# A feed-forward layer with block products for more of its columns: gate by seven products, up plain and turned, sums chained in PSUM

## The chip, the core and the metric

One core of a Trainium2 chip runs the kernel. Five engines work in parallel, each with its own queue: TensorE (PE) does matmuls, VectorE (DVE) and ScalarE (ACT) elementwise work, GpSimd (POOL) little else than transfers here, SyncE (SP) issues the other transfers. PEld is PE's loading of weights into the array. The metric is device time in microseconds (us) for one execution; smaller is better.

## The reference

256 tokens with 1024 features pass a decoder block: a gated linear recurrence and an attention, each projected, multiplied by a sigmoid gate and added, then an output projection and a SwiGLU feed-forward layer with 2816 hidden columns. The change touches the branch gates and the feed-forward layer:

```python
    gates = jax.nn.sigmoid(gl.reshape(B, S, N_BRANCH, D))      # gl: 2048 columns of h @ w_in
    merged = gates[:, :, 0, :] * y_hg + gates[:, :, 1, :] * y_at
    x = x + merged @ w_out[l]
    h2 = rmsnorm(x, ffn_norm_g[l])
    x = x + (jax.nn.silu(h2 @ w_ffn_gate[l]) * (h2 @ w_ffn_up[l])) @ w_ffn_down[l]
```

All inputs are float32.

## The kernel before

**Three matmuls for one.** A float32 product is made of fp32r parts. Every weight chunk of 128 x 2048 floats (1 MB) comes by SP into `wraw` (or a `W` tile), ACT casts it to `whi` (L55), DVE subtracts to get the rest, `wlo` (L56). PE then adds activation-high x whi, activation-high x wlo and activation-low x whi. `wraw`, `whi` and `wlo` have three buffers each (pool `wp`), used in turn by all chunks of the kernel, so the chunk after next is the furthest that can be prepared.

**Two layouts of a product.** *Feature-major* (`feat_steps`, L101 to L105): weights stand in the array, the tokens stream; high and low parts of the activations stream in one matmul of 512 columns, plus one of 256 with wlo. The result has features on partitions, as the down projection needs it; low and high sums are folded by an ACT copy of 256 and a DVE add of 256 (`fold`, L121 and L122). *Token-major*: activations stand in the array, 512 weight columns stream; the result has tokens on partitions, and for the down projection it is transposed on PE (`turn`, four transposes a quarter) and split again.

**Seven products instead of eight** (`scheme`). Tokens are cut into two halves of 128, the 1024 inputs into two of 512, 1024 columns into two of 512. A product of 2 x 2 blocks takes seven block products instead of eight, with sums of token blocks (`token_sums2`) and of weight quarters W11, W12, W21, W22 (DVE rows of 128 x 2048: L841, L848, L853, L859). A block product is 12 matmuls (L645). The results are added into the quarters `q(i, j)` by DVE.

**The feed-forward layer before.** 22 tiles of 128 hidden columns. Tiles 0 to 13 (`NPL = 14`) are plain and feature-major, in blocks of 4, 4, 4 and 2 (`plain`, gate then up, half of the 1024 inputs a step). Tiles 14 to 21 go by `scheme`: the gate's seven products stand between the steps of the plain blocks, up's seven products between the down blocks. A down block (`down_steps`, L903 to L905) takes two tiles of the hidden layer: one 1 MB chunk of w_down and 24 matmuls into four PSUM banks that add up over eleven blocks.

**The order of work.** A scheduler that builds the program places each instruction on its engine's queue; `tc.issue_after` ties a step to the last matmul of the step before it (`step`), so PE's order is that of the code. DVE and ACT get their rows in the order that the scheduler found. The branch gates are made in the same way earlier, by a `scheme` written out by hand (L701 to L735) between the steps of `at_block`.

Of the kernel before, what the change touches and what calls it, by code (L numbers as in the profile page):

```python
# [7 lines left out]
F32 = mybir.dt.float32  # L8
# [3 lines left out]
OP = mybir.AluOpType  # L12
# [15 lines left out]
def tile_hgrn2_moba_block(ctx: ExitStack, tc: tile.TileContext, xm, xw, table, runs,  # L28
# [666 lines left out]
    def gq(i, j):  # L695
        return G[0][:, i, j * 512:(j + 1) * 512]
# [4 lines left out]
    nc.scalar.copy(gq(1, 0), b1)  # L701
# [3 lines left out]
    at = then(product, b3, summed(0), halves(W11), True)  # L705
    W22 = quarter(1, 1, "T8")
# [4 lines left out]
    put_oT(halved[-1][0], low)  # L711
    b2 = pa("b2")
    at = then(product, b2, summed(1), halves(W11), True)
    W21 = quarter(1, 0, "T2")
    at = then(product, b1, tokens(0, 1), halves(W21), False)
    sigmoid(0, 0, b1)
    step1, out1 = at_block(1)
    at = then(step1)
    with tc.issue_after(halved[-1][1].ins):
        out0()  # L720
        nc.vector.tensor_add(gq(0, 1), b2, gq(1, 0))
    at = then(product, b2, summed(2), halves(W12), False)
    nc.vector.tensor_add(gq(1, 1), b2, gq(1, 0))
    nc.vector.tensor_add(gq(1, 1), gq(1, 1), b3)
# [55 lines left out]
    NPL = 14  # L780
    SC = NPL * P

    def token_sums2():
        C = big.tile([P, 4, 4, P], F32, name="C2", tag="T3")
        hi = big.tile([P, 4, 4, P], F32R, name="C2h", tag="T4")
        lo = big.tile([P, 4, 4, P], F32R, name="C2l", tag="T5")
        nc.vector.tensor_add(C[:, 0], x2f[:, 0, :, P:S], x2f[:, 1, :, P:S])
        nc.vector.tensor_sub(C[:, 1], C[:, 0], x2f[:, 0, :, 0:P])
        nc.vector.tensor_sub(C[:, 2], x2f[:, 0, :, 0:P], x2f[:, 0, :, P:S])
        nc.vector.tensor_sub(C[:, 3], x2f[:, 1, :, 0:P], C[:, 1])  # L790
# [8 lines left out]
    def plain(f0, nf, b):  # L799
        cw = nf * P  # L800
        pg = [pw() for _ in range(nf)]
        steps = feat_steps(pg, w_gate, f0 * P, x2T, cw)
        next(steps)
        yield
        next(steps)
        zt = big.tile([P, 4, S], F32, name="zt", tag=("T12", "T13")[b % 2])
        for j in range(nf // 2):
            z = zt[:, 2 * j:2 * j + 2, :]
            for i in range(2):
                fold(z[:, i, :], pg[2 * j + i])  # L810
# [9 lines left out]
        hT = big.tile([P, nf, 2, S], F32R, name="hT", tag=("T7", "T2", "T3", "T12")[b])  # L820
        for j in range(nf // 2):
            js = slice(2 * j, 2 * j + 2)
            for i in range(2 * j, 2 * j + 2):
                fold(fl[:, i, :], pu[i])
            nc.vector.tensor_mul(zt[:, js, :], zt[:, js, :], fl[:, js, :])
            split(zt[:, js, :], hT[:, js, 0, :], hT[:, js, 1, :])
        for j in range(nf):
            hk.append((f0 + j, hT, j))
        yield

    def scheme(w, banks, p1, at_out, q):
# [8 lines left out]
        nc.scalar.copy(p1, b1)  # L840
# [5 lines left out]
        b3 = banks()  # L846
# [6 lines left out]
        nc.vector.tensor_sub(W12, W22, W12)  # L853
# [20 lines left out]
    def down_steps():  # L874
        (fa, act, ja), (fb, act_b, jb) = hk[2 * chunk[0]:2 * chunk[0] + 2]
        assert fb == fa + 1 and act is act_b
# [4 lines left out]
        for tb in range(2):  # L881
            for half in range(2):
                ts = slice(tb * P, (tb + 1) * P)
                cs = slice(half * 512, (half + 1) * 512)
                if end and tb == 1 and half == 1:
                    for c0, cw in ((512, 256), (768, 256)):
                        bank = pw()
                        for i in range(2):
                            j = ja + i
                            for m, w in ((0, hi), (0, lo), (1, hi)):  # L890
                                tail[0] = nc.tensor.matmul(bank[:, 0:cw], act[:, j, m, ts], w[:, i, c0:c0 + cw],
# [7 lines left out]
                for i in range(2):  # L899
                    j = ja + i  # L900
                    st = n == 0 and i == 0
                    en = i == 1 and n == NFT // 2 - (2 if tb == 1 and half == 1 else 1)
                    nc.tensor.matmul(acc[tb][half], act[:, j, 0, ts], hi[:, i, cs], start=st, stop=False)  # L903
                    nc.tensor.matmul(acc[tb][half], act[:, j, 0, ts], lo[:, i, cs], start=False, stop=False)  # L904
                    tail[0] = nc.tensor.matmul(acc[tb][half], act[:, j, 1, ts], hi[:, i, cs], start=False, stop=en)  # L905
# [14 lines left out]
    sG = big.tile([P, 2, D], F32, name="sG", tag="T6")  # L920

    def gq2(i, j):
        return sG[:, i, j * 512:(j + 1) * 512]

    def silu(i, j, src):
        nc.scalar.activation(gq2(i, j), src, AF.Silu, scale=r2[:, i:i + 1])

    ring = iter([pa, ph, pa])
    blocks = iter([c for b in range(3) for c in [plain(4 * b, 4, b)]])
    chunks_a = (c for g in blocks for c in g)  # L930
    gate = scheme(w_gate, lambda: next(ring)("g"), gq2(1, 0), silu, gq2)
    third, chunk_no = None, 0
    for what in "cccsPcPccPcPccPcPcPc":
        if what == "c":
            with tc.issue_after(x2_split[0].ins), tc.issue_after(x2_split[1].ins):
                step(next, chunks_a) if chunk_no == 2 else None
            if chunk_no != 2:
                step(next, chunks_a)
            third = third or (halved[-1] if chunk_no == 2 else None)
            chunk_no += 1  # L940
            continue
        with tc.issue_after(third[0].ins), tc.issue_after(third[1].ins):
            if what == "P":
                step(next, gate)
            else:
                sums2 = token_sums2()
    assert not list(chunks_a) and not list(gate)
    rest = plain(12, 2, 3)
    for _ in range(4):
        step(next, rest)  # L950

    U = None
    hq = [None, None]

    def uq(i, j):
        return U[:, i, j * 512:(j + 1) * 512]

    def hidden(i, j, src):
        nc.vector.tensor_mul(uq(i, j), src, gq2(i, j))

    def turn(i, j):
        bank = pw("turn")
        src = uq(i, j)
        for k in range(4):
            tail[0] = nc.tensor.transpose(bank[:, k * P:(k + 1) * P], src[:, k * P:(k + 1) * P], ident)
        ts = slice(i * P, (i + 1) * P)
        split(bank.rearrange("p (k t) -> p k t", k=4), hq[j][:, :, 0, ts], hq[j][:, :, 1, ts])

    acc = [[ph("acc00"), ph("acc01")], [pa("acc10"), pa("acc11")]]
    p1u = big.tile([P, 512], F32, name="p1u", tag="T15")  # L970
    up = scheme(w_up, pw, p1u, hidden, uq)
    step(down)
    step(next, up)
    step(down)
    U = big.tile([P, 2, D], F32, name="U", tag="T7")
    step(next, up)
    step(down)
    step(next, up)
    step(down)
# [11 lines left out]
    parts = down_steps()
    for k in range(4):
        step(next, parts)
        if k == 2:
            step(turn, 0, 1)
    assert not list(parts)
    for j in (1, 0):
        for k in range(4):
            hk.append((NPL + 4 * j + k, hq[j], k))
    step(turn, 1, 0)  # L1000
    for _ in range(4):
        step(down)
# [45 lines left out]
```

## Time and profile before

| | |
|---|---|
| median of 3 runs | 490.17 us (490.13 to 490.63) |
| the profiled execution | 490.14 us |
| its span in the profile | 488.4 us |
| TensorE clock granted | 1.00 throughout |
| matmul instructions in the profile | 2598 |
| DMA | 91.16 MB, mean 187 GB/s |

The profile gives the busy time of each engine, a chain of work that ended last, and groups of instructions with their count, their busy time, the mean of one in ns, and the idle time of the engine ahead of them with what ended it. L12 is line 12 of the kernel. In rows by window there stand, for each engine, its busy time and the count of its instructions, then the granted clock, the share of DMA and GB/s. The feed-forward layer runs from about 305 us to the end.

### The profile page before, as it was taken

Reading aid. Unit: us, or ns where it says so; the run is one execution under the profiler, and the core shown is the slowest. Engines: PE = TensorE matmul, PEld = TensorE weight load, DVE = VectorE, ACT = ScalarE, POOL = GpSimd, SP = SyncE. Lnnn points to the kernel's source line nnn. Section 1 sums busy time; section 2 is a strip of 40 time slices with the busy share of each in tenths; the row PEclk is TensorE's granted clock in tenths of the full one; section 3 lists DMA queues with packets and bytes.
Section 4 is the critical chain, followed back from the end, with each engine's and each line's share of the span. In section 5 each row is a group of like instructions: output and inputs, shape, how many; then the busy total and the mean of one; then the engine's idle time right before and its main releaser. Section 6 shows DMA issues by size and latency. Waiting matters only on the chain.

```text
span 488.4 us, 6511 instructions
## 1 busy us (share of the span) xinstructions
PE 483.1 (99%) x2598; PEld 406.7 (83%) x2598; DVE 397.8 (81%) x426; ACT 301.7 (62%) x402; POOL 25.2 (5%) x59
## 2 busy tenths in 40 slices
PE   8999999999999999999999999999999999999997
PEld 7888888888888888988888878888888888888885
DVE  5769999697779989499987767899998779986843
ACT  5887656767748984875564445886566576444520
POOL 1930320000000000000000000000000000000000
PEclk9999999999999999999999999999999999999999
DMA  8977695624524348418267577715395664242402
GB/s 314 401 240 253 196 299 187 224 87 158 190 83 158 134 139 269 166 46 299 90 233 281 172 260 260 251 37 183 128 338 179 178 250 171 92 173 86 172 1 86
DMA packets 42142, 91.16 MB, mean 187 GB/s; under 512 B 1656, under 2 KB 3960, under 8 KB 42112
## 3 DMA queue, kind: packets, MB, share of 16 engines
q1 hardware_dynamic: 41376, 88.11, 52.5%
q0 software_dynamic: 736, 2.65, 1.7%
q8 instruction: 20, 0.33, 0.3%
q14 instruction: 10, 0.08, 0.1%
HBM read 89.67 MB, written 1.07 MB: 186 GB/s over the span
## 4 chain that ended last, share of the span: by engine, by line
PE 96%; DVE 2%; DMA 1%; issue 0%; ACT 0%
PE pw L102 16%; PE pw L84 10%; PE pw L85 10%; PE pw L86 10%; PE pw L168 5%; PE pw L105 4%; PE acc L903 4%; PE acc L905 4%; PE acc L904 4%; PE pw L101 4%; PE pw L645 4%; PE b L645 4%; PE g L645 3%; PE pw L684 1%; PE pw L685 1%; PE pw L683 1%
## 5 line engine op out<-in xcount | busy, mean ns | idle before, releaser
L56 DVE TENSOR_TENSOR wlo<-wraw,whi 128x2048 fp32r<-128x2048 f32 (+1 forms) x69 | 148.9, 2163 | 37.7 <-ACT whi L55 37.4
L55 ACT CAST whi<-wraw 128x2048 fp32r<-128x2048 f32 (+1 forms) x69 | 124.8, 1813 | 62.1 <-PE pw L86 25.2
L102 PE MATMUL pw<-x2T,whi 128*128 128x512 f32 x224 | 71.8, 395 | 0.0
L55 ACT CAST whi<-W 128x2048 fp32r<-128x2048 f32 x21 | 40.2, 1915 | 28.5 <-PE acc L905 13.6
L84 PE MATMUL pw<-whi,XT 128*128 128x512 f32 x144 | 56.9, 395 | 0.0
L56 DVE TENSOR_TENSOR wlo<-W,whi 128x2048 fp32r<-128x2048 f32 x21 | 47.9, 2286 | 10.2 <-ACT whi L55 10.1
L86 PE MATMUL pw<-whi,XT 128*128 128x512 f32 x144 | 56.2, 390 | 0.0
L85 PE MATMUL pw<-wlo,XT 128*128 128x512 f32 x144 | 56.1, 390 | 0.0
L102 PE MATMUL pw<-XT,whi 128*128 128x512 f32 x128 | 40.6, 395 | 0.0
L102 PEld LDWEIGHTS pw<-x2T,whi 128*128 128x128 f32 x224 | 35.0, 189 | 0.4
L86 PEld LDWEIGHTS pw<-whi,XT 128*128 128x128 f32 x144 | 27.0, 188 | 5.7
L84 PEld LDWEIGHTS pw<-whi,XT 128*128 128x128 f32 x144 | 27.0, 188 | 5.6
L105 PE MATMUL pw<-x2T,wlo 128*128 128x256 f32 x112 | 31.3, 279 | 0.3 <-DVE wlo L56 0.3
L85 PEld LDWEIGHTS pw<-wlo,XT 128*128 128x128 f32 x144 | 27.1, 188 | 5.4
L101 PE MATMUL pw<-x2T,wlo 128*128 128x256 f32 x112 | 31.2, 279 | 0.0
L105 PEld LDWEIGHTS pw<-x2T,wlo 128*128 128x128 f32 x112 | 21.1, 188 | 5.2 <-DVE wlo L56 0.7
L101 PEld LDWEIGHTS pw<-x2T,wlo 128*128 128x128 f32 x112 | 21.0, 188 | 5.0
L903 PE MATMUL acc<-whi,hT 128*128 128x512 f32 x56 | 21.9, 391 | 0.0
L905 PE MATMUL acc<-whi,hT 128*128 128x512 f32 x56 | 21.8, 390 | 0.0
L904 PE MATMUL acc<-wlo,hT 128*128 128x512 f32 x56 | 21.8, 389 | 0.0
L102 PEld LDWEIGHTS pw<-XT,whi 128*128 128x128 f32 x128 | 19.8, 189 | 0.2
L168 PE MATMUL pw<-whi,XT 128*128 128x512 f32 x64 | 17.6, 393 | 0.3 <-ACT whi L182 0.3
(357 smaller groups left out, 1019.9 us busy)
## 6 DMA issues: line engine op xcount, KB each, us to landing
wraw<-w_in SPq DMA_DIRECT2D x26, 1024.0 KB, 5.1
wraw<-w_down SPq DMA_DIRECT2D x11, 1024.0 KB, 5.0
wraw<-w_gate SPq DMA_DIRECT2D x6, 1024.0 KB, 5.1
wraw<-w_up SPq DMA_DIRECT2D x6, 1024.0 KB, 5.1
wraw<-w_at SPq DMA_DIRECT2D x4, 1024.0 KB, 6.6
W<-w_in SPq DMA_DIRECT2D x4, 1024.0 KB, 5.2
wraw<-w_hg SPq DMA_DIRECT2D x4, 1024.0 KB, 6.6
W<-w_gate SPq DMA_DIRECT2D x4, 1024.0 KB, 6.1
```

Of the source, the lines that this page charges most:

```text
L55: high = nc.scalar.copy(hi, src)
L56: return high, nc.vector.tensor_sub(lo, src, hi.bitcast(F32))
L84: nc.tensor.matmul(ps[tb], part(act, kt, 0)[:, ts], wh, start=(kt == 0), stop=False)
L85: nc.tensor.matmul(ps[tb], part(act, kt, 0)[:, ts], wl, start=False, stop=False)
L86: nc.tensor.matmul(ps[tb], part(act, kt, 1)[:, ts], wh, start=False, stop=(kt == KT - 1))
L101: nc.tensor.matmul(ps[ct][:, 0:S], lo[:, i, cs], part(act, kt, 0), start=False, stop=False)
L102: wide = nc.tensor.matmul(ps[ct], hi[:, i, cs], both, start=(kt == 0), stop=(kt == KT - 1))
L105: tail[0] = nc.tensor.matmul(ps[ct][:, 0:S], lo[:, i, cs], part(act, kt, 0), start=False, stop=False)
L168: nc.tensor.matmul(ps[tb], part(XT, kt, am)[:, tb * P:(tb + 1) * P], w[:, i, hs], start=(kt == 0 and am == 0 and w is wh), stop=(kt == KT ...
L645: mm = nc.tensor.matmul(bank, act(kt, m), h[:, kt, :], start=(first and kt == 0 and m == 0 and h is hi), stop=(kt == 3 and m == 1), skip_g ...
L903: nc.tensor.matmul(acc[tb][half], act[:, j, 0, ts], hi[:, i, cs], start=st, stop=False)
L904: nc.tensor.matmul(acc[tb][half], act[:, j, 0, ts], lo[:, i, cs], start=False, stop=False)
```

## The change

*Branch gates.* The same seven products at the same places. Two of them now add onto a PSUM bank that still holds an earlier product (`b1`, with `first` False), and ACT copies the bank out between; DVE has three adds in place of five, ACT two copies more.

*Feed-forward layer.* Plain and feature-major are now tiles 0 to 5 (`NPL = 6`, blocks of 4 and 2). Tiles 6 to 13 ("B", 1024 columns): gate by `scheme`, up plain but token-major (`up_plain`, four token blocks of 24 matmuls), multiplied (`times`) and turned (`turn`). Tiles 14 to 21 ("A"): gate and up by `scheme`, as before, but gate too now stands among the down blocks, and runs of up to three products stand between two down blocks ("PdPPdPPPdP", "PdPPPdP").

*The scheme itself.* The sums of weights and tokens have other signs, so that b1 adds up over products 4, 6 and 7 (`summed(1)`, `summed(2)`, `tokens(1, 1)`); three weight sums on DVE (W11+W12 L841, W11+W22 L852, W21+W11 L860) in place of four, three adds into q in place of five. W12+W22 is made by an adding transfer on POOL's queue (L842), which reads W22 from HBM a second time. Signs are put right in the scale of Silu (`r2n`) and in a multiply with -1 (L934).

```diff
-    NPL = 14
+    NPL = 6
...
-    def scheme(w, banks, p1, at_out, q):
+    def scheme(w, c0, bank, at_out, q):
...
         product(b1, tokens(0, 0, X), halves(W11), True)
-        nc.scalar.copy(p1, b1)
-        nc.vector.tensor_sub(W11, W12, W11)
+        nc.scalar.copy(q(0, 0), b1)
+        nc.vector.tensor_add(W11, W11, W12)
+        nc.gpsimd.dma_start(W12, w[512:D, c0 + 512:c0 + D].rearrange("(k p) c -> p k c", p=P), accum_op=OP.add)
         yield
-        product(b1, tokens(0, 1, X), halves(W21), False)
-        at_out(0, 0, b1)
+        b2 = bank("b2")
+        product(b2, tokens(0, 1, X), halves(W21), True)
+        nc.vector.tensor_add(q(0, 0), q(0, 0), b2)
+        at_out(0, 0, q(0, 0))
         yield
...
         product(b3, summed(0, sums2), halves(W11), True)
-        nc.vector.tensor_sub(W11, W22, W11)
+        nc.scalar.copy(q(1, 1), b3)
+        nc.vector.tensor_add(W11, W11, W22)
         yield
-        b2 = banks()
-        product(b2, summed(1, sums2), halves(W11), True)
-        nc.vector.tensor_add(q(0, 1), b2, p1)
-        nc.vector.tensor_sub(W12, W22, W12)
-        yield
-        product(b2, summed(2, sums2), halves(W12), False)
-        nc.vector.tensor_add(q(1, 1), b2, p1)
-        nc.vector.tensor_add(q(1, 1), q(1, 1), b3)
-        at_out(1, 1, q(1, 1))
-        nc.vector.tensor_sub(W21, W21, W11)
+        product(b1, summed(1, sums2), halves(W11), False)
+        nc.scalar.copy(q(0, 1), b1)
         yield
         product(b3, summed(3, sums2), halves(W22), False)
         nc.vector.tensor_add(q(0, 1), q(0, 1), b3)
         at_out(0, 1, q(0, 1))
+        nc.vector.tensor_add(W21, W21, W11)
         yield
-        product(b2, tokens(1, 1, X), halves(W21), False)
-        nc.vector.tensor_add(q(1, 0), b2, p1)
-        at_out(1, 0, q(1, 0))
+        product(b1, summed(2, sums2), halves(W12), False)
+        nc.vector.tensor_add(q(1, 1), q(1, 1), b1)
+        at_out(1, 1, q(1, 1))
+        yield
+        product(b1, tokens(1, 1, X), halves(W21), False)
+        at_out(1, 0, b1)
         yield
...
+    def up_plain(c0, q):
+        for j in range(2):
+            ps = [pw(), pw()]
+            for kt, wh, wl in chunks(w_up, c0 + j * 512, 512, (4, 4)):
+                for tb in range(2):
+                    ts = slice(tb * P, (tb + 1) * P)
+                    nc.tensor.matmul(ps[tb], part(x2T, kt, 0)[:, ts], wh, start=(kt == 0), stop=False)
+                    nc.tensor.matmul(ps[tb], part(x2T, kt, 0)[:, ts], wl, start=False, stop=False)
+                    tail[0] = nc.tensor.matmul(ps[tb], part(x2T, kt, 1)[:, ts], wh, start=False, stop=(kt == KT - 1))
+                if kt == 3:
+                    yield
+            for tb in range(2):
+                nc.scalar.copy(q(tb, j), ps[tb])
+            yield
...
+    step(next, second_c)
+    step(next, second_c)
+    step(next, gate)
+    UB = quarters("UB", "T7")
+    up_b = up_plain(FB * P, UB)
+    step(next, up_b)
+    step(next, gate)
...
+    for what in "PdPPdPPPdP":
+        step(*((down,) if what == "d" else (next, gate)))
...
+    for what in "PdPPPdP":
+        step(*((down,) if what == "d" else (next, up)))
+    hA1 = turned2(FA + 4, "T2")
+    hA0 = turned2(FA, "T3")
+    step(turn, UA, 0, 0, *hA0, banks["b2"])
+    step(next, up)
+    step(turn, UA, 0, 1, *hA1)
+    step(down)
+    step(turn, UA, 1, 1, *hA1, banks["b3"])
```

How this moves rows is seen in the order of the built programs. First place: DVE's queue in the first gate scheme, from the wlo of its third product on (before: `wlo_2986`; W00 to W11 are the quarters W11 to W22, zt the folded gate of a plain block):

```order
L56 TENSOR_TENSOR wlo_2986<-W00_2793,whi_2985 128x2048
L56 TENSOR_TENSOR wlo_3008<-wraw_3006,whi_3007 128x2048
L122 TENSOR_TENSOR zt_2971<-pw_2891,zt_2971 128x256
L122 TENSOR_TENSOR zt_2971<-pw_2892,zt_2971 128x256
L122 TENSOR_TENSOR zt_2971<-pw_2893,zt_2971 128x256
L811 TENSOR_TENSOR zt_2971<-zt_2971,R2_2636 128x512
L122 TENSOR_TENSOR zt_2971<-pw_2894,zt_2971 128x256
L848 TENSOR_TENSOR W00_2793<-W11_2799,W00_2793 128x2048
```

The changed kernel, from the wlo of the third product (`wlo_2951`) to that of the first token block of up (`wlo_2973`) and one further:

```order
L56 TENSOR_TENSOR wlo_2951<-W00_2795,whi_2950 128x2048
L56 TENSOR_TENSOR hT_2862<-zt_2729,hT_2862 128x2x256
L852 TENSOR_TENSOR W00_2795<-W00_2795,W11_2801 128x2048
L122 TENSOR_TENSOR zt_2942<-pw_2896,zt_2942 128x256
L122 TENSOR_TENSOR zt_2942<-pw_2897,zt_2942 128x256
L56 TENSOR_TENSOR wlo_2973<-wraw_2971,whi_2972 128x2048
L810 TENSOR_TENSOR zt_2942<-zt_2942,R2_2636 128x512
```

The next chunk's wlo stood directly behind the third product's; now an hT row, the weight sum L852 and two folds stand between them.

Second place: DVE's queue in the up scheme, from the wlo of the third product to that of the fourth. Before, with a down block's wlo (`wlo_3630`) among them:

```order
L56 TENSOR_TENSOR wlo_3612<-W00_3505,whi_3611 128x2048
L959 TENSOR_TENSOR U_3562<-pw_3513,sG_2646 128x512
L848 TENSOR_TENSOR W00_3505<-W11_3511,W00_3505 128x2048
L56 TENSOR_TENSOR wlo_3630<-wraw_3628,whi_3629 128x2048
L859 TENSOR_TENSOR W10_3507<-W10_3507,W00_3505 128x2048
L56 TENSOR_TENSOR wlo_3661<-W00_3505,whi_3660 128x2048
```

In the changed kernel (the third product's is `wlo_3600`, the fourth's `wlo_3618`; the gate scheme of the same columns has the same rows, with a down block's wlo as the last):

```order
L56 TENSOR_TENSOR wlo_3600<-W00_3521,whi_3599 128x2048
L852 TENSOR_TENSOR W00_3521<-W00_3521,W11_3527 128x2048
L860 TENSOR_TENSOR W10_3523<-W10_3523,W00_3521 128x2048
L846 TENSOR_TENSOR UA_3520<-UA_3520,b2_3579 128x512
L56 TENSOR_TENSOR wlo_3618<-W00_3521,whi_3617 128x2048
```

Both weight sums stood a down block's wlo apart; now they follow each other, with an add into q, ahead of the next wlo.

Third place: the turn of the quarter (0, 1) of up. On PE before (`turn_3833`, inside a down block):

```order
L905 MATMUL acc10_3472<-whi_3810,hT_3462 128x512
L903 MATMUL acc10_3472<-whi_3810,hT_3462 128x512
L904 MATMUL acc10_3472<-wlo_3811,hT_3462 128x512
L905 MATMUL acc10_3472<-whi_3810,hT_3462 128x512
L965 MATMUL turn_3833<-ident_268,U_3562 128x128 x4
L903 MATMUL acc11_3473<-whi_3810,hT_3462 128x512
```

and now (`turn_3709`, between the last matmuls of the sixth product and a down block):

```order
L645 MATMUL b1_3529<-whi_3691,C2h_2785 128x512
L645 MATMUL b1_3529<-wlo_3692,C2h_2785 128x512
L645 MATMUL b1_3529<-whi_3691,C2l_2786 128x512
L960 MATMUL turn_3709<-ident_268,UA_3520 128x128 x4
L902 MATMUL acc00_3242<-whi_3717,hh_3276 128x512
L903 MATMUL acc00_3242<-wlo_3718,hh_3276 128x512
```

On DVE before, from the wlo of the down block that holds the turn (`wlo_3811`) on: L862 adds into U(0, 1), the L959 row behind the next wlo multiplies it by the gate:

```order
L56 TENSOR_TENSOR wlo_3811<-wraw_3809,whi_3810 128x2048
L862 TENSOR_TENSOR U_3562<-U_3562,pw_3610 128x512
L56 TENSOR_TENSOR wlo_3855<-wraw_3853,whi_3854 128x2048
L959 TENSOR_TENSOR U_3562<-U_3562,sG_2646 128x512
L56 TENSOR_TENSOR hq1_3765<-turn_3784,hq1_3765 128x4x128
```

and now, from the wlo of the down block that follows the turn on PE (`wlo_3718`; L858 adds into the quarter, `wlo_3753` is the seventh product's, L934 multiplies by the gate):

```order
L56 TENSOR_TENSOR wlo_3718<-wraw_3716,whi_3717 128x2048
L858 TENSOR_TENSOR UA_3520<-UA_3520,b3_3598 128x512
L56 TENSOR_TENSOR wlo_3753<-W10_3523,whi_3752 128x2048
L934 SCALAR_TENSOR_TENSOR UA_3520<-UA_3520,GA_3292 128x512
L56 TENSOR_TENSOR hq_3684<-b2_3579,hq_3684 128x4x128
```

The turn moved from the last quarter of a down block to the front of one; on DVE a wlo stands between the add and the multiply, before and now.

More of the change, by code (lines that the diff above doesn't have):

```diff
@@ L699, in sigmoid @@
         nc.scalar.activation(gq(i, j), src, AF.Sigmoid, scale=rx[:, i:i + 1])
-    nc.scalar.copy(gq(1, 0), b1)
+    nc.scalar.copy(gq(0, 0), b1)
     nc.vector.tensor_sub(W11, W12, W11)
@@ L705, in tile_hgrn2_moba_block @@
     at = then(product, b3, summed(0), halves(W11), True)
+    nc.scalar.copy(gq(1, 1), b3)
     W22 = quarter(1, 1, "T8")
@@ L711, in tile_hgrn2_moba_block @@
     put_oT(halved[-1][0], low)
+    at = then(product, b1, summed(1), halves(W11), False)
+    nc.scalar.copy(gq(0, 1), b1)
+    W21 = quarter(1, 0, "T2")
     b2 = pa("b2")
[L713 to L716, printed above, removed]
+    at = then(product, b2, tokens(0, 1), halves(W21), True)
     step1, out1 = at_block(1)
@@ L720, in tile_hgrn2_moba_block @@
         out0()
[L721 to L724, printed above, removed]
+        nc.vector.tensor_add(gq(0, 0), gq(0, 0), b2)
+    sigmoid(0, 0, gq(0, 0))
+    at = then(product, b1, summed(2), halves(W12), False)
+    nc.vector.tensor_add(gq(1, 1), gq(1, 1), b1)
     sigmoid(1, 1, gq(1, 1))
@@ L732, in tile_hgrn2_moba_block @@
     sigmoid(0, 1, gq(0, 1))
-    at = then(product, b2, tokens(1, 1), halves(W21), False)
-    nc.vector.tensor_add(gq(1, 0), b2, gq(1, 0))
-    sigmoid(1, 0, gq(1, 0))
+    at = then(product, b1, tokens(1, 1), halves(W21), False)
+    sigmoid(1, 0, b1)
     M = [big.tile([P, 4, 2, S], F32R, name=f"M{i}", tag=("T8", "T9")[i]) for i in range(2)]
@@ L918, in down @@
             pass
[L920 to L926, printed above, removed]
-    ring = iter([pa, ph, pa])
[L929 to L967, printed above, removed]
+    r2n = small.tile([P, 2], F32, name="r2n")
@@ new lines, in tile_hgrn2_moba_block, with quarters, gate_scheme, at_out @@
+    nc.vector.tensor_scalar_mul(r2n, r2, -1.0)
+    def quarters(name, tag):
+        t = big.tile([P, 2, D], F32, name=name, tag=tag)
+        return lambda i, j: t[:, i, j * 512:(j + 1) * 512]
+    def gate_scheme(c0, bank, q):
+        def at_out(i, j, src):
+            nc.scalar.activation(q(i, j), src, AF.Silu, scale=(r2, r2n)[j][:, i:i + 1])
+        return scheme(w_gate, c0, bank, at_out, q)
+    def up_scheme(c0, bank, q, g):
+        def at_out(i, j, src):
+            if j:
+                nc.vector.scalar_tensor_tensor(q(i, j), src, -1.0, g(i, j), op0=OP.mult, op1=OP.mult)
+            else:
+                nc.vector.tensor_mul(q(i, j), src, g(i, j))
+        return scheme(w_up, c0, bank, at_out, q)
@@ new lines, in times, with turn, turned @@
+    def times(i, j):
+        nc.vector.tensor_mul(UB(i, j), UB(i, j), GB(i, j))
+    def turn(q, i, j, hi, lo, bank=None):
+        bank = bank or pw("turn")
+        for k in range(4):
+            tail[0] = nc.tensor.transpose(bank[:, k * P:(k + 1) * P], q(i, j)[:, k * P:(k + 1) * P], ident)
+        ts = slice(i * P, (i + 1) * P)
+        split(bank.rearrange("p (k t) -> p k t", k=4), hi[:, :, ts], lo[:, :, ts])
+    def turned(f0, tags):
+        t = [big.tile([P, 4, S], F32R, name="hh", tag=g) for g in tags]
+        for k in range(4):
+            hk.append((f0 + k, lambda m, ts, k=k: t[m][:, k, ts]))
+        return t
@@ new lines, in turned2 @@
+    def turned2(f0, tag):
+        t = big.tile([P, 2, 4, S], F32R, name="hq", tag=tag)
+        for k in range(4):
+            hk.append((f0 + k, lambda m, ts, k=k: t[:, m, k, ts]))
+        return t[:, 0], t[:, 1]
+    FB, FA = NPL, NPL + 8
+    GB = quarters("GB", "T6")
+    ring = iter([pa, ph, pa])
+    gate = gate_scheme(FB * P, lambda name: next(ring)(name), GB)
+    first_c, second_c = plain(0, 4, 0), plain(4, 2, 1)
+    for k in range(2):
+        step(next, first_c)
+    with tc.issue_after(x2_split[0].ins), tc.issue_after(x2_split[1].ins):
+        step(next, first_c)
@@ new lines, in tile_hgrn2_moba_block @@
+    third = halved[-1]
+    with tc.issue_after(third[0].ins), tc.issue_after(third[1].ins):
+        sums2 = token_sums2()
+        step(next, gate)
+        step(next, first_c)
+        step(next, gate)
+    step(next, second_c)
+    step(next, second_c)
+    step(next, gate)
+    UB = quarters("UB", "T7")
+    up_b = up_plain(FB * P, UB)
+    step(next, up_b)
+    step(next, gate)
+    step(next, up_b)
+    step(next, gate)
+    times(0, 0)
+    step(next, second_c)
+    step(next, second_c)
@@ L969, in tile_hgrn2_moba_block @@
+    step(next, gate)
+    step(next, up_b)
+    step(next, gate)
+    times(1, 0)
+    hB0 = turned2(FB, "T3")
+    step(turn, UB, 0, 0, *hB0)
+    step(next, up_b)
+    assert not list(up_b) and not list(gate) and not list(first_c) and not list(second_c)
+    times(0, 1)
+    times(1, 1)
+    step(turn, UB, 1, 0, *hB0)
     acc = [[ph("acc00"), ph("acc01")], [pa("acc10"), pa("acc11")]]
-    p1u = big.tile([P, 512], F32, name="p1u", tag="T15")
-    up = scheme(w_up, pw, p1u, hidden, uq)
     step(down)
+    hB1 = turned(FB + 4, ("T13", "T15"))
@@ L987, in tile_hgrn2_moba_block @@
-    step(next, up)
-    step(turn, 1, 1)
+    step(turn, UA, 1, 1, *hA1, banks["b3"])
     step(next, up)
     assert not list(up)
[L991 to L1001, printed above, removed]
+    step(down)
+    step(turn, UA, 1, 0, *hA0, banks["b2"])
+    for _ in range(3):
```

61 lines of the change are left out of this document (29 added, 32 removed).

## The prediction, made before the changed kernel was run

> **What bounds the kernel now.** I read the page first: busy shares and the chain that ended last.
>
> ```profile
> span 488.4 us, 6511 instructions
> PE 483.1 (99%) x2598; PEld 406.7 (83%) x2598; DVE 397.8 (81%) x426; ACT 301.7 (62%) x402; POOL 25.2 (5%) x59
> PE 96%; DVE 2%; DMA 1%; issue 0%; ACT 0%
> ```
>
> PE carries 96% of the chain. But matmuls overlap, so a busy PE would also show through short waits. Second, therefore, the windows of PE alone between the starts of its groups; the count includes the first matmul of the next group.
>
> ```profile
> 322.73:325.47 2.74, 2.74 (x13) 1.00 0.00 0
> 325.47:331.64 6.17, 5.88 (x34) 1.00 0.54 170
> 334.36:345.50 11.14, 11.14 (x65) 1.00 0.46 156
> 409.13:411.85 2.72, 2.72 (x13) 1.00 0.00 0
> 411.85:417.29 5.44, 5.44 (x25) 1.00 0.59 193
> 441.78:442.13 0.35, 0.35 (x5) 1.00 1.19 82
> ```
>
> These are prices: a block product (12 matmuls) 2.72 us, a down block (24 matmuls) 5.44, 64 feature-major matmuls (32 wide, 32 narrow) 11.14, a turn of four transposes 0.35. The second row is 32 feature-major matmuls, half of 11.14 or 5.57, in 6.17: PE waited 0.60 us there. Elsewhere in the feed-forward part the groups stand at their price. So PE's work sets the time, and DVE is the engine close behind it, as windows of all engines show (PE, PEld, DVE, ACT, POOL):
>
> ```profile
> 322.73:345.50 22.77, 22.48 (x121) 19.06 (x120) 22.17 (x21) 14.30 (x17) 0.00 (x0) 1.00 0.43 139
> 403.69:430.00 26.31, 26.31 (x118) 21.79 (x117) 25.14 (x16) 14.35 (x10) 0.00 (x0) 1.00 0.42 145
> ```
>
> DVE was busy 22.17 of 22.77 us and 25.14 of 26.31 us, and PE lost 0.60 us in the one and nothing in the other. What decides is thus the order in which DVE's queue holds its work. Third, the timeline of DVE and ACT, which shows how a weight chunk gets ready:
>
> ```profile
> 410.98 0.68 DVE L56 TENSOR_TENSOR hT<-zt,hT 128x512 fp32r<-128x512 f32 x1
> 411.59 2.28 DVE L56 TENSOR_TENSOR wlo<-W,whi 128x2048 fp32r<-128x2048 f32 x1
> 413.79 2.29 DVE L853 TENSOR_TENSOR W<-W,W 128x2048 f32<-128x2048 f32 x1
> 415.99 2.28 DVE L56 TENSOR_TENSOR wlo<-wraw,whi 128x2048 fp32r<-128x2048 f32 x1
> 419.44 2.29 DVE L56 TENSOR_TENSOR wlo<-W,whi 128x2048 fp32r<-128x2048 f32 x1 [1.17 <-ACT whi L55]
> 412.05 0.59 ACT L840 COPY p1u<-pw 128x512 f32<-128x512 f32 x1 [0.72 <-PE pw L645]
> 412.54 1.92 ACT L55 CAST whi<-wraw 128x2048 fp32r<-128x2048 f32 x1
> 417.49 1.92 ACT L55 CAST whi<-W 128x2048 fp32r<-128x2048 f32 x1 [3.04 <-PE acc L905]
> ```
>
> Queued DVE rows start 2.20 us apart (411.59, 413.79, 415.99), a 512 row takes 0.61 of the queue (410.98 to 411.59): the rows overlap by 0.08. An ACT copy takes 0.49 of its queue. The last cast waited for the down block that ended at 417.29: there are three buffers of whi and of wlo, so a chunk's cast starts 0.20 us after PE has left the chunk three before it, and its wlo 0.03 after the cast's end (417.49 + 1.92 = 419.41). From a freed buffer to a finished wlo are 0.20 + 1.92 + 0.03 + 2.28 = 4.43 us, if ACT and DVE come at once. PE needs wlo at its second matmul.
>
> **The change part by part.** *Branch gates (first half of the diff).* The same products stand at the same places on PE. DVE loses two PSUM adds, ACT gains two copies.
>
> ```profile
> 239.00 0.68 DVE L721 TENSOR_TENSOR G<-b,G 128x512 f32<-128x512 f32 x1
> L701 ACT COPY G<-b 128x512 f32<-128x512 f32 x1 | 0.6, 585 | 0.2 <-PE b L645 0.2
> ```
>
> PE has the chain there; the copies of 0.59 go ahead of weight casts whose products come a product or more later (2.72 us), and DVE's 1.36 us were no one's wait. I take 0; without that cover each copy would cost 0.5.
>
> *PE's work.* Two plain blocks of four tiles go, gate and up: 256 feature-major matmuls, 4 x 11.14 = 44.56. Added: seven products, 19.04; four token blocks of 24 matmuls at the down block's price, 21.76; four turns, 1.40. Sum 42.20: **-2.36 us**.
>
> *The wait of 0.60.* A W subtraction of 2.28 (L841) stood in front of the second up chunk's wlo. In the changed order both wlo rows precede the addition. I take **-0.60**, at worst 0.
>
> *Four new waits.* I walk DVE's queue at the places where PE has the least lead. Other prices (mean ns):
>
> ```profile
> L122 DVE TENSOR_TENSOR zt<-pw,zt 128x256 f32<-128x256 f32 x14 | 5.4, 416 | 0.6 <-ACT zt L121 0.5
> L56 DVE TENSOR_TENSOR hT<-zt,hT 128x512 fp32r<-128x512 f32 x7 | 4.7, 684 | 0.1
> L908 DVE SCALAR_TENSOR_TENSOR x<-acc,r,x 128x512 f32<-128x512 f32 x3 | 2.3, 751 | 1.8 <-PE acc L905 1.8
> ```
>
> Less the 0.08: a fold 0.33, a 512 row 0.60, the multiply with a scalar 0.67. The last row of each walk has its full length (+0.08), and PE restarts 0.05 later.
>
> (a) First token block of up, in the first gate scheme. From the end of PE's second product: ACT and start 2.15 (0.20 + 1.92 + 0.03); wlo of the third product 2.20, hT 0.60, W11+W22 2.20, two folds 0.66, wlo of the token block 2.20 + 0.13. It is ready at 10.14. PE meanwhile has two narrow blocks (5.57), the third product (2.72) and two matmuls with whi (0.45): 8.74. **Wait 1.40.** DVE must be free at that start, and its queue is full from the third split of the stage on:
>
> ```profile
> 309.53 2.29 DVE L56 TENSOR_TENSOR wlo<-wraw,whi 128x2048 fp32r<-128x2048 f32 x1 [1.11 <-ACT whi L55]
> L56 DVE TENSOR_TENSOR wlo<-wraw,whi 128x1024 fp32r<-128x1024 f32 x8 | 9.7, 1224 | 4.3 <-ACT whi L55 4.1
> ```
>
> From 309.53 to the third product's wlo stand five 2048 rows (11.0), four of 1024 at 1.14 (4.6), eight of 512 (4.8), two with a scalar (1.3), nine folds and the like (3.0) and some 0.6 of small ones: 25.3, to 334.8. PE's second product ends at 322.73 + 2.74 + 5.57 + 2.72 = 333.8, its successor's cast at 335.9. So DVE is there with 1.1 to spare.
>
> (b) Gate of the last columns. From the end of its first product: 0.20, ACT's copy 0.49, cast and start 1.95; wlo of the third product 2.20, W11+W22 2.20, W21+W11 2.20, the add into q 0.60, wlo of the down block 2.20 + 0.13: 12.17. PE: down block 5.44, two products 5.44, one matmul 0.23: 11.11. **Wait 1.06.**
>
> (c) The up scheme of the same columns has the same five DVE rows before its fourth product; PE again a down block and two products. **Wait 1.06.**
>
> (d) The turn of U(0,1) is now placed right behind the sixth product. From the end of the down block before the fifth: 2.15; wlo of the next down block 2.20, add into q 0.60, wlo of the seventh product 2.20, multiply by the gate 0.67 + 0.13: 7.95. PE: product, turn, product, 5.79. **Wait 2.16**: the down block behind the turn has its chunk, but stands in PE's queue behind it.
>
> Sum +5.68. None depends on the sums of the others: each starts from an end on PE. (d) rests on DVE keeping its order, which rows show: an hq subtraction whose cast ended at 444.37 (443.79 + 0.58) stood until 446.13 behind a wlo that DVE had first waited for.
>
> ```profile
> 443.79 0.58 ACT L55 CAST hq<-turn 128x512 fp32r<-128x512 f32 x1
> 443.92 2.29 DVE L56 TENSOR_TENSOR wlo<-W,whi 128x2048 fp32r<-128x2048 f32 x1 [3.07 <-ACT whi L55]
> 446.13 0.68 DVE L56 TENSOR_TENSOR hq<-turn,hq 128x512 fp32r<-128x512 f32 x1
> ```
>
> The Trainium skill has this as a rule that speaks against the change (TensorE: Matmul & The Clock Gate, the section on the array's architectural detail): "ACT/DVE are strict FIFO", and this trace agrees.
>
> *W12+W22 by an adding transfer on POOL's queue.* It takes three W rows (2.28 each) off DVE; that is in the walks. The trace has no adding transfer. The nearest rows are plain ones of the same size (us to landing):
>
> ```profile
> x<-xm POOLq DMA_DIRECT2D x1, 1024.0 KB, 5.2
> W<-w_up SPq DMA_DIRECT2D x4, 1024.0 KB, 5.3
> ```
>
> POOL has nothing else queued. Issue follows W11+W12 after the first product; the sum is first cast before the sixth. In the up scheme, the tightest, PE has in between two down blocks and four products less the lead of three chunks: about 19 us. Price 0 up to 19 us to landing, then 1 us each; it cannot gain. I take 0, as 5.2 is nearest.
>
> *The end.* Three down blocks follow the last turn as before: 0.
>
> Against the profiled execution (490.14 us; span 488.4; median 490.17): 490.14 - 2.36 - 0.60 + 5.68 = **492.9 us**, slower. Each wait is uncertain by some 0.3, the part that goes by 0.6.
>
> **The rivals.**
>
> *PE keeps its pace* (the other side): the casts and the W additions come early enough and no new wait arises: 490.14 - 2.96 = 487.2. For it: PE lost only 0.60 us with DVE 95 to 97% busy, and DVE's work hardly grows. Against: every walk begins at a buffer freed by PE, which nothing can advance. It decides once all four chains are 1.1 to 2.2 us shorter. 0.14.
>
> *Half the waits*: (d) falls away, or (b) and (c), because rows behind a waiting one go ahead. If DVE's queue let ready rows pass, (b), (c) and (d) would all go and 490.14 - 2.96 + 1.40 = 488.6 stay; with only (d) gone, 490.7. The rows at 443.92 and 446.13 speak against it. 0.11.
>
> *DVE falls further behind*: from the token sums to the first token block its queue has little slack, and a delay there goes on into (a) and the blocks after it. One W row more in each scheme's waits, 2.2, gives 495.1. For it: 22.17 of 22.77 us busy; against: the 1.1 us to spare in (a). 0.09.
>
> *The adding transfer is late* in one scheme: at five times the plain price, 26 us, 7 us late there: about 500. For it only that no row shows one. 0.03.
>
> **How the numbers follow.** The forecast has 0.63, its own range 491.7 to 494.1 (four waits, 0.3 each, adding up, without part of the 0.60). The 8-in-10 range takes in half the waits and DVE's further fall: 489.6 to 495.1; PE at its pace and the late transfer, 0.17, stay out. A measurement of this kernel tells about 0.2% (1 us) from no change: faster (below 489.2) 0.16, from the first rival and a little of the second; same 0.09; slower 0.75.
>
> **What would show it.** Right: PE waits of 1 to 2 us for DVE wlo at the first token matmul of up, at the third down block and at the fourth product of the last up scheme, and for DVE's multiply at the turn of U(0,1); 60 matmuls fewer; no wait at 325; no row waiting for the POOL transfer. Wrong: PE's groups at their prices throughout, or long waits of ACT's cast for the transferred W12.

## The result, and the profile after

493.78 us median (493.38 to 493.95, 4 runs) against 490.33 (490.13 to 490.63, 4 runs): ratio 1.0069, 95% interval 1.0051 to 1.0086. The change makes the kernel 3.45 us slower; by the prediction's sum it was to be 2.72. The profiled execution took 493.61, span 491.9.

The page of after: the span, the engines, the chain that ended last.

```profile
span 491.9 us, 6402 instructions
PE 482.4 (98%) x2538; PEld 404.0 (82%) x2538; DVE 397.7 (81%) x408; ACT 308.7 (63%) x402; POOL 29.1 (6%) x62
PE 90%; DVE 6%; ACT 2%; issue 1%; ACTq 0%
```

60 matmuls fewer, yet the span is longer, and DVE's share of the chain has grown from 2% to 6%. Who lets PE wait stands in the waits of PE's weight loads (total, times, longest):

```profile
PEld turn L960 <- DVE UA L934: 2.2, 1, 2.2
PEld pw L946 <- DVE wlo L56: 1.7, 1, 1.7
PEld b L645 <- DVE wlo L56: 1.6, 1, 1.6
PEld acc L903 <- DVE wlo L56: 0.9, 1, 0.9
```

These are the four places of the forecast. These rows count the waits of weight loads; what PE itself lost is read from the windows below. The row for the old wait, which this view had in the kernel before, is gone:

```profile
PEld pw L105 <- DVE wlo L56: 0.7, 1, 0.7
```

The windows of PE between group starts give their net lengths (the second row is the first token block, then the third down block, the three products with the fourth among them, the sixth product, the seventh product; the last two rows are a down block behind a turn and one behind a product):

```profile
325.55:331.12 5.57, 5.57 (x33) 1.00 0.89 231
342.14:349.19 7.05, 5.74 (x26) 1.00 0.26 74
402.90:409.15 6.25, 5.77 (x25) 1.00 0.60 195
433.63:443.25 9.62, 8.46 (x37) 1.00 0.22 77
451.77:456.59 4.82, 3.02 (x15) 1.00 0.49 150
462.94:465.79 2.85, 2.85 (x15) 1.00 0.92 365
382.81:388.40 5.59, 5.59 (x28) 1.00 0.23 29
392.02:397.46 5.44, 5.44 (x25) 1.00 0.64 221
```

The first row is the place of the old wait, now at its price. (a) 7.05 - 5.44 = 1.61; (b) 6.25 - 5.44 = 0.81; (c) 9.62 - 3 x 2.72 = 1.46; (d) 4.82 - 2.85 = 1.97, since a product behind a turn takes 2.85 (sixth row). Together 5.85. (b), which the prediction's signs put at 1 to 2 us, is below that. The whole feed-forward stretch, from its first matmul to the start of the last, before and after:

```profile
304.70:484.54 179.84, 179.54 (x913) 1.00 0.45 155
```

```profile
304.77:488.01 183.24, 178.49 (x853) 1.00 0.54 170
```

It grew by 3.40. Less 5.85, plus the 0.60 that went, PE's own work fell by 1.85 us, where 2.36 were forecast. This 1.85 is what remains of the sum, not a measurement of its own.

### The profile page after: what moved, and what is told of

It reads as the page before. It is cut to its first block, busy times and chain, and to the rows that moved or that the text cites. A ratio compares the mean times of both kernels' runs of the same rounds, so it can differ in the third digit from the quotient of the medians.

```text
span 491.9 us, 6402 instructions
## 1 busy us (share of the span) xinstructions
PE 482.4 (98%) x2538; PEld 404.0 (82%) x2538; DVE 397.7 (81%) x408; ACT 308.7 (63%) x402; POOL 29.1 (6%) x62
## 3 DMA queue, kind: packets, MB, share of 16 engines
q0 software_dynamic: 2320, 5.79, 5.4%
## 4 chain that ended last, share of the span: by engine, by line
PE 90%; DVE 6%; ACT 2%; issue 1%; ACTq 0%
PE b L645 12%; PE pw L102 10%; PE pw L84 10%; PE pw L86 10%; PE pw L85 10%; PE pw L168 5%; DVE wlo L56 3%; PE acc L903 3%; PE acc L904 3%; PE acc L902 3%; PE pw L101 2%; PE pw L105 2%; ACT whi L55 2%; PE pw L946 2%; PE pw L947 1%; PE pw L684 1%
## 5 line engine op out<-in xcount | busy, mean ns | idle before, releaser
L56 DVE TENSOR_TENSOR wlo<-W,whi 128x2048 fp32r<-128x2048 f32 x28 | 63.9, 2288 | 10.2 <-ACT whi L55 10.0
L55 ACT CAST whi<-W 128x2048 fp32r<-128x2048 f32 x28 | 53.6, 1914 | 28.2 <-PE acc L904 6.9
L102 PE MATMUL pw<-XT,whi 128*128 128x512 f32 x128 | 40.6, 395 | 0.0
L102 PE MATMUL pw<-x2T,whi 128*128 128x512 f32 x96 | 31.0, 396 | 0.0
L645 PE MATMUL b<-whi,x2T 128*128 128x512 f32 x72 | 23.7, 392 | 0.0
L102 PEld LDWEIGHTS pw<-XT,whi 128*128 128x128 f32 x128 | 19.8, 189 | 0.2
L645 PE MATMUL b<-wlo,C2h 128*128 128x512 f32 x48 | 18.8, 391 | 1.2 <-DVE wlo L56 1.2
L645 PE MATMUL b<-whi,C2h 128*128 128x512 f32 x48 | 18.8, 392 | 0.0
L645 PE MATMUL b<-whi,C2l 128*128 128x512 f32 x48 | 18.7, 390 | 0.0
L902 PE MATMUL acc<-whi,hq 128*128 128x512 f32 x46 | 18.0, 392 | 0.0
L903 PE MATMUL acc<-wlo,hq 128*128 128x512 f32 x46 | 17.9, 390 | 0.0
L904 PE MATMUL acc<-whi,hq 128*128 128x512 f32 x46 | 17.9, 389 | 0.0
L101 PE MATMUL pw<-XT,wlo 128*128 128x256 f32 x64 | 17.8, 279 | 0.0
```

The lines of the kernel that those rows point to most:

```text
L55: high = nc.scalar.copy(hi, src)
L56: return high, nc.vector.tensor_sub(lo, src, hi.bitcast(F32))
L101: nc.tensor.matmul(ps[ct][:, 0:S], lo[:, i, cs], part(act, kt, 0), start=False, stop=False)
L102: wide = nc.tensor.matmul(ps[ct], hi[:, i, cs], both, start=(kt == 0), stop=(kt == KT - 1))
L645: mm = nc.tensor.matmul(bank, act(kt, m), h[:, kt, :], start=(first and kt == 0 and m == 0 and h is hi), stop=(kt == 3 and m == 1), skip_g ...
L902: nc.tensor.matmul(acc[tb][half], act[i](0, ts), hi[:, i, cs], start=st, stop=False)
```

## The experiments

Each was timed beside the kernel before on the same chip (490.2 to 490.5). "Less" and "more" compare with the 493.78 of after, so one or two tenths of a microsecond mean nothing. Line numbers are those of each kernel.

**One wait alone, (d).** The turn goes into the down block, as it stood before.

```diff
-    step(turn, UA, 0, 1, *hA1)
-    step(down)
+    parts = down_steps()
+    for k in range(4):
+        step(next, parts)
+        if k == 2:
+            step(turn, UA, 0, 1, *hA1)
```

> The changed kernel with the turn of U(0,1) put inside the down block that it stood ahead of, after its third quarter. Nothing else moves but DVE's two rows that depend on it: the wlo of the next down block now stands ahead of the multiply with the gate. Theory (the four waits come from the order of DVE's queue and each is worth its own length): the wait of 2.19 at the turn goes, no other comes, 493.8 - 2.0 = 491.8, interval about 491.4 to 492.2. Rival A (DVE is simply short of time, as its load is what it was): the 2 us reappear at the next weight chunk, 493.5 to 493.8. Rival B (the adding transfers slow everything a little): 493.8.

491.78 us, ratio 1.0028 (1.0017 to 1.0038): 2.00 less than after. The 2.2 us at L934 are gone from PE's waits, and the three others stand as they were. At the next turn a weight load now waits 0.3 for L934, of which PE loses 0.06 (that turn takes 0.41 instead of 0.35). The 2 us did not reappear at the next chunk: rival A, which takes DVE's load for the cause, fails here.

**(b) and a part of (c).** W21+W11 behind the next wlo.

```diff
-        nc.vector.tensor_add(W21, W21, W11)
+        with tc.issue_after(halved[-1][1].ins):
+            nc.vector.tensor_add(W21, W21, W11)
```

> The changed kernel with the row W21+W11 (2.20 of DVE's queue) put behind the wlo of the following product in all three schemes; W21 isn't needed before two products later. Theory: the wait at the third down block (gate of the last columns, 0.8) goes whole, since the wlo of that block then stands right behind W11+W22; of the wait at the fourth product of the last up scheme (1.45) about 0.8 stays, because the add into q that waits for the second product now stands ahead of that wlo: 8.16 + 0.20 + 0.60 + 0.60 + 2.33 = 11.89 after the first product's end against PE's 11.11. Together -1.5: 492.3. Rival A (DVE's load): the row still has to run, the waits move one chunk on, 493.8. Rival B (transfers): 493.8.

492.88 us, ratio 1.0049 (1.0036 to 1.0061): 0.90 less. PE's waits in the feed-forward part are now three:

```profile
PEld turn L961 <- DVE UA L935: 2.2, 1, 2.2
PEld pw L947 <- DVE wlo L56: 1.7, 1, 1.7
PEld b L645 <- DVE wlo L56: 1.2, 1, 1.2
```

(b) went whole (0.81). Of (c) only 0.4 went, not 0.7: a row of 2.20 taken out of DVE's queue shortened the wait by a fifth of it. (Together that is 1.2, and the time fell by 0.90. The first product of the feed-forward part started 0.5 later here than in after; over the profiled runs up to the fifth experiment that start lies between 322.5 and 323.6.) Something other than the queue carries most of the rest; the fifth experiment shows what.

**(a), by another order on PE.** The token block ahead of gate's third product.

```diff
-    step(next, gate)
     UB = quarters("UB", "T7")
     up_b = up_plain(FB * P, UB)
     step(next, up_b)
     step(next, gate)
+    step(next, gate)
```

> The changed kernel with the first token block of up placed ahead of the third product of gate in the first scheme, so that the block's wlo does not stand behind W11+W22. Theory: the wait at the token block (1.6) goes; but W21+W11 now stands ahead of the wlo of the fourth product, which may wait up to 1.8 there (walk 15.8 against 13.96 from the end of the second product). So 492.2 if that cover holds, 494.0 if not, and in that case the trace shows the wait at the fourth product. Rival A (DVE's load): 493.8 with the wait spread. Rival B (transfers): 493.8 with the wait at the token block still there.

493.50 us, ratio 1.0064 (1.0050 to 1.0078): hardly a gain. The trace shows why: L946's wait is gone, and PE's waits for a product have become two, 3.2 us in all.

```profile
PEld b L645 <- DVE wlo L56: 3.2, 2, 1.7
```

The wait moved to the fourth product, as the second case of the expectation had it: what is taken from one walk was laid on the next.

**All three.**

> The three edits together: turn inside the down block, W21+W11 behind the next wlo, the token block first. With W21+W11 out of the way the fourth product of the first scheme has about 0.3 to spare. Theory: of the four waits (5.8) only some 0.8 at the fourth product of the last up scheme stays: 493.8 - 5.0 = 488.8, below the kernel before (490.3), since the 2.96 of the change's PE work are then seen. Rival A (DVE's load): 492 to 493.8. Rival B (transfers cost in the background): no better than 490.3.

489.88 us, ratio 0.9989 (0.9980 to 0.9998): 3.90 less than after and, barely, faster than before. Two waits are left, at the fourth product of the first scheme and of the last (2.1, 2 times). The first was not expected.

**The rows left in front of them.** The second product's add and output go behind the fourth product's wlo.

```diff
         product(b2, tokens(0, 1, X), halves(W21), True)
-        nc.vector.tensor_add(q(0, 0), q(0, 0), b2)
-        at_out(0, 0, q(0, 0))
         yield
...
         product(b1, summed(1, sums2), halves(W11), False)
+        with tc.issue_after(halved[-1][1].ins):
+            nc.vector.tensor_add(q(0, 0), q(0, 0), b2)
+            at_out(0, 0, q(0, 0))
```

> The kernel with the three edits, and the second product's add into q and its output (one row of DVE, one of ACT) put behind the wlo of the fourth product. What was left there of the waits are 0.8 at the fourth product of the first scheme and 1.0 at that of the last up scheme. Theory (each such wait is a chain that begins at a buffer freed by PE, and gets shorter by every row taken out of it): 0.6 to 0.7 goes at each, 489.9 - 1.3 = 488.6. Rival A (DVE's load, which is unchanged): 489.9. Rival B (the rows now stand ahead of the next wlo and cost the same there): 489.9 with new waits a product later.

489.43 us, ratio 0.9977 (0.9968 to 0.9986): 0.45 less, a third of what was expected, and no new wait. My theory was too simple here. The timelines of DVE and of ACT in this kernel, first scheme:

```profile
338.71 2.29 DVE L56 TENSOR_TENSOR wlo<-W,whi 128x2048 fp32r<-128x2048 f32 x1
340.92 0.75 DVE L122 TENSOR_TENSOR zt<-pw,zt 128x256 f32<-128x256 f32 x2
341.58 2.28 DVE L850 TENSOR_TENSOR W<-W,W 128x2048 f32<-128x2048 f32 x1
345.90 2.29 DVE L56 TENSOR_TENSOR wlo<-W,whi 128x2048 fp32r<-128x2048 f32 x1 [1.43 <-ACT whi L55]
348.11 0.68 DVE L854 TENSOR_TENSOR GB<-GB,b 128x512 f32<-128x512 f32 x1
```

```profile
336.75 1.91 ACT L55 CAST whi<-W 128x2048 fp32r<-128x2048 f32 x1 [0.37 <-PE pw L102]
343.95 1.91 ACT L55 CAST whi<-W 128x2048 fp32r<-128x2048 f32 x1 [4.09 <-DVE W L850]
```

DVE was idle for 1.43 us just before the late wlo. The fourth product's chunk W11+W22 is made from the third's in place: it can be added only when the third's wlo is done (338.71 + 2.29), cast only when it is added (343.86), split only when it is cast. That is a chain of data through DVE, ACT and DVE, begun by a buffer that PE frees (the cast at 336.75 waited for L102). Rows that stand beside this chain cost nothing as long as they leave it room. In the first scheme only the two folds (0.66) still stand in it; in the last up scheme nothing but the chain is left.

**The chain given room.** The folds go behind W11+W22, and in the last up scheme the second down block goes ahead of the fourth product, which the chain feeds, no longer behind it. (Two steps that only place the folds aren't shown.)

```diff
+        with tc.issue_after((w_sum[-1] if b else tail[0]).ins):
             for j in range(nf // 2):
...
-        nc.vector.tensor_add(W11, W11, W22)
+        w_sum.append(nc.vector.tensor_add(W11, W11, W22))
...
-    for what in "PdPPPdP":
+    for what in "PdPPdPP":
```

> The last kernel with two more edits: in the first scheme the folds of the narrow gate block stand behind W11+W22 in DVE's queue (0.66 out of the chain from the freed buffer to the fourth product's wlo), and in the last up scheme the second down block stands between the fourth and the fifth product's old place, that is behind the fourth product's predecessor no longer: the order P d P P P d P becomes P d P P d P P, so that the chain wlo, W11+W22, cast, wlo has 5.44 more to run in. Theory: the two waits left (0.68 and 0.65) go, 489.4 - 1.3 = 488.1, and PE has no wait for DVE left in the feed-forward part. Rival (DVE's load, or the fifth product's chunk is now late instead): 489.4, with a wait at the fifth or sixth product.

488.08 us, ratio 0.9952 (0.9939 to 0.9966): 5.70 less than after, as expected, and 2.25 less than before. The longest weight-load wait for DVE that is left in the feed-forward part:

```profile
PEld b L645 <- DVE wlo L56: 0.3, 1, 0.3
```

DVE's work is that of after (408 instructions, 397.8 us busy against 397.7): so the 5.7 us were order, and none of it load. (The string puts that down block between the third and the fourth product, where it had stood between the fourth and the fifth; the expectation says this less clearly.)

**The adding transfer.** Left out, so that W12 lacks W22:

```diff
-        nc.gpsimd.dma_start(W12, w[512:D, c0 + 512:c0 + D].rearrange("(k p) c -> p k c", p=P), accum_op=OP.add)
```

> The changed kernel without the three adding transfers: the addition of W22 to W12 is left out, 3 MB of traffic and POOL's issues with it. Nothing else moves. Theory (the transfers have some 19 us and more of cover and cost nothing): 493.8, within 0.3. Rival B (they slow the weight loads or the engines in the background, or the cast of W12 waits for them): 493.2 or less; at most the four waits, 488.

494.00 us, ratio 1.0069 (1.0055 to 1.0083), the four waits unchanged. Its price is 0.

**The addition on DVE instead.** The same line becomes `nc.vector.tensor_add(W12, W12, W22)`.

> The changed kernel with W12+W22 added by DVE at the place of the transfer, three rows of 2.20 more in DVE's queue and three transfers less. Theory (DVE's order decides, and the transfer is free): in the last up scheme the row stands ahead of the wlo of the down block that begins at 428.19, which ends at 429.1 instead of 426.9: 0.7 more. In the first scheme it delays the wlo of the first token block, whose queue had about 1.1 to spare, by 1.1 to 2.8 more; in the gate of the last columns it fits. 495.6 to 497.3. Rival B (the transfers cost something themselves): 493.8 or less. If DVE had time to spare anyway: 493.8.

496.44 us, ratio 1.0124 (1.0110 to 1.0138): 2.66 more. The wait at (a) grew from 1.7 to 2.9, and small ones came at the third product of the first scheme and at the down block of the last up scheme. Here a DVE row costs time, since it stands in the walks. So the transfer brings what it was priced at, DVE rows out of the walks, for nothing.

**The branch half alone**, in the kernel before.

> The kernel before with the first half of the change alone: the branch gates' sums chained in PSUM, the feed-forward part as before. Theory (two DVE rows less and two copies of 0.59 more on ACT, all beside PE's work): 490.3, within 0.3. Rival C (the copies delay weight casts there, and part of the 3.45 us comes from this half): 490.8 to 491.3, with PE waits between 190 and 290 us.

490.51 us, ratio 1.0001 (0.9992 to 1.0010). Price 0, as forecast.

**What a turn costs.** Idle transposes in the last three down blocks of after; first one behind every third matmul, 22 in all:

```diff
+                    if spare:
+                        nc.tensor.transpose(spare[0][:, 0:P], ident, ident)
```

> The changed kernel with 22 single transposes of the identity into a bank that nobody reads, one behind every third matmul in the last three down blocks (the last quarter left out), where nothing else waits. It measures what a transpose between matmuls costs. If it is its own 0.11 each, as the turns' pace inside a turn: 22 x 0.11 = 2.4, 496.2. Theory (each passage from matmuls to transposes and back costs about 0.14 more, as the groups behind a turn look: 2.86 instead of 2.72): 22 x 0.25 = 5.5, 499.3. In that case the four turns that the change adds cost 0.5 to 0.6 more than the 1.40 put down for them.

496.42 us, 2.64 more than after: 0.12 each. The theory of a passage that costs 0.14 beyond the transpose fails. Then whole turns, four transposes behind every sixth matmul, eleven in all:

> The changed kernel with eleven idle turns (four transposes of the identity into a bank that nobody reads), one behind every six matmuls of the last three down blocks but for the last quarter. It measures a whole turn, as the prediction priced it. At the 0.35 put down for a turn, from its first start to the next matmul's start: 11 x 0.35 = 3.9, 497.7. By the single transposes just measured (0.12 for the first, 0.11 for each that follows): 11 x 0.45 = 4.9, 498.7. By the groups behind the turns of this kernel, which are 0.15 longer (5.59 instead of 5.44): 11 x 0.50 = 5.5, 499.3.

498.80 us, 5.02 more: 0.456 a turn, the middle case. The prediction's 0.35 ran from a turn's first start to the next matmul's start. The transposes start 0.11 apart, but the matmul behind the last one starts 0.03 after it and is itself followed 0.32 later instead of 0.23: most of the last transpose's time lies in the group behind, and the window missed it.

## Why the prediction was right, and where its sizes were off

**Branch gates**, 0: shown (490.51 against 490.46). **The old wait**, -0.60: gone whole. **The adding transfer**, 0: shown, though it took about twice the plain time that I leaned on (below). **The end**, 0: three down blocks follow the last turn, without a wait for DVE.

**PE's work**, -2.36: -1.85 in the runs. The mis-sized step is "four turns, 1.40": at 0.456 they are 1.82, which explains 0.42 of the 0.51. Read from after itself, where one of them stands ahead of a token block, one ahead of a down block (5.59 above) and two together ahead of a product, they come to a little more:

```profile
376.53:376.88 0.35, 0.35 (x6) 1.00 0.94 386
376.88:382.46 5.58, 5.58 (x28) 1.00 0.73 266
388.40:389.19 0.79, 0.79 (x10) 1.00 1.11 205
389.19:392.02 2.83, 2.83 (x15) 1.00 1.13 209
```

0.35 + 0.14, 0.35 + 0.15 and 0.79 + 0.11 are 1.89, 0.49 of the 0.51. The kernel of 488.08 gives nearly the same by another road:

```profile
304.90:482.49 177.59, 177.59 (x852) 1.00 0.55 175
```

Its feed-forward stretch is 177.59, of which 0.29 are what is left of the waits (a pair of products in 5.65, a token block in 5.52). Against the 179.84 of before, less the old wait of 0.60, PE's work is shorter by 1.94.

**The four waits**, +5.68: measured 5.85, at the four places. (a), (b) and (d) each went with the edit made for it, (c) shrank with two edits and went when its chain got room. That the sum is so near is partly luck: the parts are off by 0.21, -0.25, 0.40 and -0.19.

- (a) 1.40, measured 1.61. PE's first matmul that has waited for DVE is followed 0.34 later instead of 0.23, at all three wlo places: 0.11 that no walk had (404.45 to 404.79 below is one).
- (b) 1.06, measured 0.81, from errors of opposite sign. I let PE need wlo at its second matmul. In this block four matmuls with whi come first, 0.68 us more lead:

```profile
402.90 1.07 PE L902 MATMUL acc<-whi,hT 128*128 128x512 f32 x4
404.45 0.50 PE L903 MATMUL acc<-wlo,hT 128*128 128x512 f32 x1 [0.48 <-DVE wlo L56]
404.79 0.40 PE L904 MATMUL acc<-whi,hT 128*128 128x512 f32 x1
```

  Against that, DVE was slower than my walk, as in (c), and the 0.11 came on top.
- (c) 1.06, measured 1.46. The rows of DVE in after:

```profile
430.83 2.29 DVE L56 TENSOR_TENSOR wlo<-W,whi 128x2048 fp32r<-128x2048 f32 x1 [0.34 <-ACT whi L55]
433.15 2.29 DVE L852 TENSOR_TENSOR W<-W,W 128x2048 f32<-128x2048 f32 x1
435.48 2.29 DVE L860 TENSOR_TENSOR W<-W,W 128x2048 f32<-128x2048 f32 x1
437.69 0.68 DVE L846 TENSOR_TENSOR UA<-UA,b 128x512 f32<-128x512 f32 x1
438.29 2.28 DVE L56 TENSOR_TENSOR wlo<-W,whi 128x2048 fp32r<-128x2048 f32 x1
```

The first two pairs start 2.32 and 2.33 apart, the third 2.21. L852 writes over what the wlo ahead of it reads, and L860 reads what L852 writes: these dependent rows do not overlap (each starts 0.03 or 0.04 after the end of the one ahead), and I had put 2.20 everywhere. That is 0.25 of the 0.40, and the 0.11 of (a) most of the rest.

- (d) 2.16, measured 1.97. DVE's rows here ran as walked, one behind the other:

```profile
453.05 0.68 DVE L858 TENSOR_TENSOR UA<-UA,b 128x512 f32<-128x512 f32 x1
453.64 2.29 DVE L56 TENSOR_TENSOR wlo<-W,whi 128x2048 fp32r<-128x2048 f32 x1
455.85 0.69 DVE L934 SCALAR_TENSOR_TENSOR UA<-UA,GA 128x512 f32<-128x512 f32 x1
```

  From the end of the down block (448.69) to the turn (456.59) they took 7.90, where 7.95 were walked. PE's side took 5.93 instead of 5.79: the product behind the turn of U(0,0) takes 2.85. So this part, too, was off by the price of a turn.

By sums: -1.85 - 0.60 + 5.85 = 3.40, and 0.07 ahead of the feed-forward part: 3.47, the profiled runs' difference.

**The rivals.** PE at its pace fails by the four rows of PE's waits. It was half right in one thing: the saving was there to be had, as 488.08 shows once the order is mended. Half the waits fails: all four stand at their places. The row that I leaned on against it decides nothing, since the wlo at 443.92 had begun before the hq cast ended at 444.37. A row of the fifth experiment does show DVE keeping its order: the add at 348.11 (L854) has the result of the second product, whose last matmul started at 333.49, and yet DVE stood idle for 1.43 us ahead of the wlo at 345.90 with this add queued behind it. In the kernel before, the multiply L691 at 237.81 stood in the same way behind an idle 1.00 us and the wlo at 235.60, though the last matmul of its product had started at 233.18. DVE further behind fails: (a) ended at 1.61, near its walk. The late transfer fails by the kernel without it.

What the walks lacked was the difference between a row in the queue and a row in the chain of data. In (c) the queue and the chain W11+W22, cast, wlo lay nearly level, so taking rows out of the queue gave back only a part. A fourth buffer of whi and wlo, which would start every walk one chunk earlier, wasn't tried.

## What to carry over

When an engine at 95% feeds one at 99%, price a change by walking the second engine's queue from the moment that the first frees a buffer, place by place; busy shares would have said nothing here. Before you move a row out of such a walk, look whether the walk is held by the queue or by a chain of data through several engines: only what stands in the longer of the two gives time back. And measure a group's price to the end of the group behind it, not to the next start.

## What the runs showed of the hardware

- The three adding transfers of 1 MB took about twice as long as the one plain transfer of that size on the same queue. DMA issues of after (KB each, median us to landing):

```profile
W<-w_gate POOLq DMA_DIRECT2D x2, 1024.0 KB, 9.5
x<-xm POOLq DMA_DIRECT2D x1, 1024.0 KB, 5.2
W<-w_up POOLq DMA_DIRECT2D x1, 1024.0 KB, 10.7
```

- A long PE wait can cost more than itself. In the kernel with the addition on DVE, a weight load waited 2.9 us for a token block's wlo; PE had no matmul running for 2.5 us of it, and the granted clock was at half for the 3.4 us behind it. Windows of PE (length, busy, clock, share of DMA, GB/s):

```profile
342.74:345.50 2.76, 0.39 (x2) 1.00 0.00 0
345.50:348.90 3.40, 3.28 (x8) 0.50 0.55 154
348.90:352.00 3.10, 3.10 (x15) 1.00 0.27 42
```

Matmuls started 0.43 apart there instead of 0.23, some 1.5 us on top of the wait. It is one execution, at 497.23 the slowest of the four timed. Its mean granted clock was 0.997; that of the other three (495.78 to 496.52) was 1.00, so the same program does not lose the clock each time, and the median of 496.44 holds none of it. After itself, with waits up to 2.2, shows 1.00 throughout these stretches. The Trainium skill (TensorE: Matmul & The Clock Gate, "Part 1: The HAM clock gate") describes a free-running activity window of about 3.4 us after which an idle array drops to half rate: the length and the half rate agree with this trace. The Trainium skill's advice to avoid idle gaps above about 3 us (TensorE: Matmul & The Clock Gate, "Why this matters for your kernels") is no safe line here, since 2.5 us without a matmul were followed by it once.
